# A fp32r decoder trunk on one core: 32 bytes more per buffer of the weights' parts and per block of the normed activations

## The chip, the core and the metric

The kernel runs on one core of one Trainium2 chip. The metric is the device time of one execution in microseconds. Before the change the median of three runs is 1750.88 us (1750.79 to 1751.33). One more execution was taken with the hardware profiler, and every row below is from it.

## The reference

Two identical layers (DEPTH = 2) on one sequence of 512 tokens, model width 1024, in float32:

```
for l in range(DEPTH):
    h = rms_norm(x, ln1[l])
    x = x + mixer_block(h, ...)      # one input projection, four token mixers, gated up-projections, w_out
    h = rms_norm(x, ln2[l])
    x = x + swiglu(h, w_ffn_in[l], w_ffn_out[l])
...
def swiglu(h, w_in, w_out):
    gate, up = jnp.split(h @ w_in, 2, axis=-1)
    return (jax.nn.silu(gate) * up) @ w_out
```

Nearly all arithmetic is in the products with weights: the input projection of 8,220 columns, the up-projections, `w_out`, and the feed-forward part with 2,816 hidden units.

## The kernel before

Activations lie transposed: 128 partitions hold 128 channels, and the 512 tokens run along the partition. A weight matrix is cut into blocks of 128 x 128, and eight blocks make a slab of 128 x 1024 float32, 4,096 bytes in each partition. SyncE's queue brings a slab into a tile `wr`. `convert` splits it into two parts: ScalarE copies it, rounded to fp32r, into `wh` (line 197), and VectorE subtracts, so that `wl` holds the rest (line 198). Activations are split in the same manner: `Norm` holds the normed activations as `xh` and `xl`, eight blocks of 512 columns each; other operands are split into tiles `t` (mixers) and `f` (feed-forward part).

Each product is three matmuls (`mm3`, all recorded under line 183): high by high, low activations by high weights, high activations by low weights. A matmul has a stationary operand, here nearly always a 128 x 128 weight block, and a moving operand, here the activations' columns. TensorE loads the stationary operand of the next matmul (a row of PEld) while the moving operand of the present one streams. For the token-major projections the roles are exchanged: blocks of `xh` and `xl` are stationary, and 256 or 284 columns of `wh` and `wl` move.

The order of the work is that of the program text with fillers pulled in between the mixers' steps, put in order once when the kernel is built. Slabs are split two ahead of their use (`AHEAD`). The first feed-forward product goes by Strassen's seven products on halves of 256 columns: the moving operands are halves of `xh` and `xl` and sums `t1`, `t2`, `t3` in tiles of their own. For three of the seven (p = 1, 2, 4) both weights' parts are in `wh` and `wl` (`wl` by an accumulating DMA from GpSimd's queue, lines 1263 and 1264). For the other four the low part is in a tile `l`.

Where a buffer lies follows from the pools, which are laid one behind the other in the order of the code, each buffer with its bytes per partition. Of the addresses, the remainder modulo 128 matters here; it is called the phase. Before the change every buffer that is named below has a length that is a multiple of 128 bytes, and so:

| buffers | role in TensorE | phase before | phase after |
|---|---|---|---|
| `wh`, three buffers | mostly stationary | 64, 64, 64 | 64, 96, 0 |
| `wl`, three buffers | mostly stationary | 64, 64, 64 | 32, 64, 96 |
| `xh`, `xl`, block k of eight | mostly moving | 64 for all k | 32k: 0, 32, 64, 96, 0, ... |
| `t`, `f`, `t1`, `t2`, `t3` | moving | 0 | 0 |
| `l` | stationary | 0 | 0 |
| `wr` | read by ScalarE, VectorE | 64 | 64 |

A block of 128 weight columns is 512 bytes, so all eight blocks of a slab have the slab's phase. Buffers rotate, so that `wl` lies 32 below its `wh` as long as both advance together.

Of the kernel before, what the change touches and what calls it, by code (L numbers as in the profile page):

```python
# [10 lines left out]
F32 = mybir.dt.float32  # L11
F32R = mybir.dt.float32r
# [6 lines left out]
P = 128  # L19
S = 512  # L20
D = 1024
KD = D // P
# [13 lines left out]
SLAB = 8  # L36
# [95 lines left out]
def trunk(ctx: ExitStack, tc: tile.TileContext, keys, qkeys, xin, pos, wst, wsq, par, ext, cst, out):  # L132
# [4 lines left out]
    wp = ctx.enter_context(tc.tile_pool(name="wp", bufs=3))  # L137
    bp = ctx.enter_context(tc.tile_pool(name="bp", bufs=1))
# [7 lines left out]
    def nm(s):  # L146
        uid[0] += 1
        return f"{s}{uid[0]}"

    pools = {}  # L150

    def phase(**bufs):
        st = ExitStack()
        for n, b in bufs.items():
            pools[n] = st.enter_context(tc.tile_pool(name=nm(n), bufs=b, reuse_waits="tile"))
        return st

    def mixers():
        return phase(gp=2, vp=2, bd=1, tp=33)
# [7 lines left out]
    def FT(shape, dtype=F32):  # L167
        return pools["fp"].tile(shape, dtype, tag="f", name=nm("f"))
# [27 lines left out]
    def split(src, hi, lo):  # L196
        A.copy(out=hi, in_=src)  # L197
        V.tensor_tensor(out=lo, in0=src, in1=hi.bitcast(F32), op=ALU.subtract)  # L198
        return hi, lo
# [38 lines left out]
    def halves(n):  # L238
        w = SLAB * P
        return [slice(0, w // 2), slice(w // 2, w)] if n < 2 else [slice(0, w)]  # L240

    def convert():
        n = len(ready)
        if n < SLABS:
            hi = wp.tile([P, SLAB * P], F32R, tag="wh", name=nm("wh"))
            lo = wp.tile([P, SLAB * P], F32R, tag="wl", name=nm("wl"))
            for h in halves(n):
                split(raw[n][:, h], hi[:, h], lo[:, h])
            ready.append((hi, lo))
            raw[n] = None  # L250

    def ahead(n):
        while len(ready) < min(SLABS, cap[0], n):
            if len(raw) == len(ready):
                load()
            convert()
# [105 lines left out]
    class Norm:  # L362
        def __init__(self, gain):
            self.gain = gain
            self.hi = bp.tile([P, KD, S], F32R, tag="xh", name=nm("xh"))
            self.lo = bp.tile([P, KD, S], F32R, tag="xl", name=nm("xl"))
            self.part = []

        def __getitem__(self, k):
# [51 lines left out]
    def layer(l, n1, scope):  # L421
# [770 lines left out]


        scope = phase(tq=1, ep=8, rp=5, lp=2, fp=9)

        last = l == DEPTH - 1
# [33 lines left out]
        def strassen(units):  # L1230
            n = len(units)
            st = [{} for _ in units]
# [8 lines left out]
            def load(u):  # L1241
                for q, (dk, dm) in (("11", (0, 0)), ("12", (HK, 0)), ("21", (0, 1)), ("22", (HK, 1))):
                    if q == "22":
                        t = wp.tile([P, SLAB * P], F32, tag="wr", name=nm("wr"), bufs=2)
                    else:
                        t = pools["rp"].tile([P, SLAB * P], F32, tag="rq", name=nm("rq"))
                    j = len(qkeys) // SLAB
                    for base in (0, FFN):
                        qkeys.extend([("w_ffn_in", l, k + dk, base + (units[u] + dm) * P) for k in range(HK)])
                    nc.sync.dma_start(out=t, in_=wsq[j])  # L1250
                    st[u][q] = t, j

            def sub(o, a, b, op=ALU.subtract):
                V.tensor_tensor(out=o, in0=a, in1=b, op=op)
                return o

            def LT():
                return pools["lp"].tile([P, SLAB * P], F32R, tag="l", name=nm("l"))

            def early(u, p):  # L1260
                t, j = st[u][OF[p]]
                lo = wp.tile([P, SLAB * P], F32R, tag="wl", name=nm("wl"))
                A.activation(out=lo, in_=t, func=AF.Copy, scale=-1.0)  # L1263
                G.dma_start(out=lo, in_=wsq[j], accum_op=ALU.add)  # L1264
                st[u]["lo", p] = lo

            def prep(u, p):
                s = st[u]
                hi = wp.tile([P, SLAB * P], F32R, tag="wh", name=nm("wh"))
                if p in LATE:  # L1270
                    A.copy(out=hi, in_=s[OF[p]][0])
                    s[p] = hi, s.pop(("lo", p))
                    return
                a11, a12, a21, a22 = (s[q][0] for q in ("11", "12", "21", "22"))
                if p == 6:
                    s1 = wp.tile([P, SLAB * P], F32, tag="wr", name=nm("wr"), bufs=2)
                    s["s1"] = sub(s1, a21, a22, ALU.add)
                    sub(a21, a11, a21)
                    sub(a11, s1, a11)
                    s[p] = split(a11, hi, LT())  # L1280
                    if u + 1 < len(units):
                        load(u + 1)
                    return
                if p == 3:
                    sub(a12, a12, a11)
                t = {5: s["s1"], 7: a21, 3: a12}[p]
                s[p] = split(t, hi, LT())
# [10 lines left out]
            def begin(i):  # L1298
                if i < 0:
                    load(0)  # L1300
                    upto("early", 2, early, lambda p: p in LATE)
                    return
                upto("prep", i + 3, prep, lambda p: True)
                upto("early", i + 6, early, lambda p: p in LATE)
# [80 lines left out]
        hi, lo = split(a, FT([P, 2, S], F32R), FT([P, 2, S], F32R))  # L1385
# [117 lines left out]
```

## Time and profile before

| | |
|---|---|
| median of three runs | 1750.88 us |
| the profiled execution, its own time | 1751.48 us |
| its span, first to last instruction | 1749.8 us |
| TensorE matmuls busy | 1736.9 us, 99% of the span |
| weight loads (PEld) busy | 1500.2 us, 86% |
| VectorE, ScalarE, GpSimd busy | 1215.5, 862.0, 225.9 us |

Matmuls are recorded with modelled ends: the recorded duration of one covers more than the time until the next starts, because they are pipelined. The time that a stream of matmuls costs is read from the starts: last start less first start, over the number of matmuls between them.

### The profile page before, as it was taken

What the parts mean: (1) busy time and instruction counts of PE and PEld (TensorE: products, weight loads), DVE (VectorE), ACT (ScalarE), POOL (GpSimd) and SP (SyncE); (2) the same over time, 40 slices, a digit from 0 to 9 for tenths busy, and PEclk for the clock granted to TensorE, in tenths of its full rate; (3) what the DMA queues carried; (4) which work ended last, traced back from release to release, by engine and by line L of the source; (5) the groups of instructions that cost most, each with busy time, mean ns of one, the idle gap of its engine ahead of it and who ended that gap; (6) DMA issues with size and microseconds to landing.
All of it is one profiled execution on the core that took longest, in us unless ns stands there. A gap on an engine that the chain in (4) does not pass through costs nothing.

```text
span 1749.8 us, 25123 instructions
## 1 busy us (share of the span) xinstructions
PE 1736.9 (99%) x10140; PEld 1500.2 (86%) x10140; DVE 1215.5 (69%) x1683; ACT 862.0 (49%) x1190; POOL 225.9 (13%) x227
## 2 busy tenths in 40 slices
PE   9999999999999999999999999999999999999998
PEld 7878888888888999898988788888888898999987
DVE  5868576777667666675777666767776685666666
ACT  5425533555347455463544254335544473645543
POOL 2032120022101000000010311201220010100000
PEclk9999999999999999999999999999999999999999
DMA  6322222222236566575333222322222365656652
GB/s 202 97 83 62 86 72 85 84 85 85 84 97 171 157 140 172 130 183 108 86 102 114 68 67 73 96 73 84 85 84 85 119 169 146 147 156 140 173 107 99
DMA packets 54693, 195.00 MB, mean 111 GB/s; under 512 B 6064, under 2 KB 6448, under 8 KB 54576
## 3 DMA queue, kind: packets, MB, share of 16 engines
q1 hardware_dynamic: 45072, 160.45, 29.0%
q0 software_dynamic: 8640, 31.46, 10.4%
q8 instruction: 79, 1.29, 0.3%
q10 hardware_dynamic: 864, 1.48, 0.2%
q14 instruction: 38, 0.31, 0.1%
HBM read 191.27 MB, written 2.10 MB: 111 GB/s over the span
## 4 chain that ended last, share of the span: by engine, by line
PE 96%; DVE 2%; DMA 1%; ACT 1%; issue 0%; ACTq 0%; DVEq 0%
PE mm L183 64%; PE mx L183 31%; DVE wl L198 1%; PE mx L1058 0%; DMA x<-in_x_dram 0%; DMA t<-in_ext_dram 0%; ACT wh L197 0%; DVE f L1399 0%; DVE x L1400 0%; PE mx L658 0%; DVE t L352 0%; ACT L216 0%; ACT g L221 0%; DVE t L1147 0%; PE mx L930 0%
## 5 line engine op out<-in xcount | busy, mean ns | idle before, releaser
L197 ACT CAST wh<-wr 128x1024 fp32r<-128x1024 f32 (+1 forms) x240 | 249.8, 1042 | 394.5 <-PE mm L183 247.7
L183 PE MATMUL mm<-xh,wh 128*128 128x512 f32 (+1 forms) x1184 | 431.4, 364 | 0.8 <-DVE t L1147 0.8
L183 PE MATMUL mm<-xh,wl 128*128 128x512 f32 (+1 forms) x1184 | 430.5, 364 | 0.0
L183 PE MATMUL mm<-xl,wh 128*128 128x512 f32 (+1 forms) x1184 | 429.8, 363 | 0.0
L198 DVE TENSOR_TENSOR wl<-wr,wh 128x1024 fp32r<-128x1024 f32 (+1 forms) x220 | 282.0, 1283 | 117.9 <-ACT wh L197 109.7
L183 PEld LDWEIGHTS mm<-xh,wh 128*128 128x128 f32 x1184 | 223.5, 189 | 36.3 <-DVE t L1147 1.7
L183 PEld LDWEIGHTS mm<-xh,wl 128*128 128x128 f32 x1184 | 223.7, 189 | 34.8 <-issue 1.5
L183 PEld LDWEIGHTS mm<-xl,wh 128*128 128x128 f32 x1184 | 223.6, 189 | 33.7 <-issue 1.1
L183 PE MATMUL mm<-t,wh 128*128 128x512 f32 x448 | 142.5, 397 | 0.0
L183 PE MATMUL mx<-xl,wh 128*128 128x256 f32 (+1 forms) x448 | 140.4, 313 | 0.0
L183 PE MATMUL mx<-xh,wh 128*128 128x256 f32 (+1 forms) x448 | 137.8, 314 | 2.3 <-ACT wh L197 2.3
L1264 POOL DMA_DIRECT2D wl<-in_wsq_dram x60 | 51.9, 864 | 542.1 <-ACT wl L1263 322.9
L183 PE MATMUL mx<-f,wh 128*128 128x512 f32 x352 | 110.2, 395 | 0.0
L183 PE MATMUL mm<-f,wh 128*128 128x512 f32 x352 | 108.3, 396 | 0.0
L183 PEld LDWEIGHTS mm<-t,wh 128*128 128x128 f32 x448 | 83.2, 188 | 19.1
L198 DVE TENSOR_TENSOR l<-rq,wh 128x1024 fp32r<-128x1024 f32 x60 | 73.2, 1220 | 34.6 <-ACT wh L197 19.1
L183 PEld LDWEIGHTS mx<-xh,wh 128*128 128x128 f32 x448 | 84.6, 189 | 8.9 <-ACT wh L197 3.5
L183 PE MATMUL mx<-xh,wl 128*128 128x256 f32 (+1 forms) x288 | 91.9, 330 | 0.0
L183 PEld LDWEIGHTS mx<-xl,wh 128*128 128x128 f32 x448 | 84.7, 189 | 5.3
L183 PE MATMUL mm<-t,wl 128*128 128x512 f32 x224 | 88.5, 395 | 0.0
L183 PEld LDWEIGHTS mm<-f,wh 128*128 128x128 f32 x352 | 65.7, 188 | 16.2 <-ACT wh L197 1.0
L183 PEld LDWEIGHTS mx<-f,wh 128*128 128x128 f32 x352 | 65.4, 188 | 15.5
(275 smaller groups left out, 3470.8 us busy)
## 6 DMA issues: line engine op xcount, KB each, us to landing
wr<-in_wst_dram SPq DMA_DIRECT2D x216, 512.0 KB, 3.5
rq<-in_wsq_dram SPq DMA_DIRECT2D x60, 512.0 KB, 4.6
wl<-in_wsq_dram POOLq DMA_DIRECT2D x60, 512.0 KB, 5.7
wr<-in_wsq_dram SPq DMA_DIRECT2D x20, 512.0 KB, 5.0
out_dram<-x SPq DMA_DIRECT2D x8, 256.0 KB, 2.0
x<-in_x_dram SPq DMA_DIRECT2D x3, 512.0 KB, 6.9
wr<-in_wst_dram SPq DMA_DIRECT2D x4, 256.0 KB, 5.4
x<-in_x_dram SPq DMA_DIRECT2D x2, 256.0 KB, 4.5
```

The costliest lines, as they stand in the source:

```text
L183: T.matmul(o, lhsT=l, rhs=r, start=start, stop=stop, skip_group_check=True)
L197: A.copy(out=hi, in_=src)
L198: V.tensor_tensor(out=lo, in0=src, in1=hi.bitcast(F32), op=ALU.subtract)
L1264: G.dma_start(out=lo, in_=wsq[j], accum_op=ALU.add)
```

## The change

Every buffer of `wh` and `wl` becomes 8 float32 (32 bytes) longer, and every block of `xh` and `xl` too; the additional elements are neither written nor read, since the slices `[:, :SLAB * P]` and `[:, :, :S]` cut them off. A tile of 64 bytes is laid in front of each phase's pools, which brings the buffers behind it back to the phase that they had. The built program has the same instructions on every engine, in the same order, with the same waits; only addresses differ.

```diff
+    def pad(pool, n):
+        pool.tile([P, n // 4], F32, tag=nm("pad"), name=nm("pad"))
+
...
     def phase(**bufs):
         st = ExitStack()
+        pad(st.enter_context(tc.tile_pool(name=nm("gap"), bufs=1)), 64)
...
     def convert():
...
-            hi = wp.tile([P, SLAB * P], F32R, tag="wh", name=nm("wh"))
-            lo = wp.tile([P, SLAB * P], F32R, tag="wl", name=nm("wl"))
+            hi = wp.tile([P, SLAB * P + 8], F32R, tag="wh", name=nm("wh"))[:, :SLAB * P]
+            lo = wp.tile([P, SLAB * P + 8], F32R, tag="wl", name=nm("wl"))[:, :SLAB * P]
...
     class Norm:
...
-            self.hi = bp.tile([P, KD, S], F32R, tag="xh", name=nm("xh"))
-            self.lo = bp.tile([P, KD, S], F32R, tag="xl", name=nm("xl"))
+            self.hi = bp.tile([P, KD, S + 8], F32R, tag="xh", name=nm("xh"))[:, :, :S]
+            self.lo = bp.tile([P, KD, S + 8], F32R, tag="xl", name=nm("xl"))[:, :, :S]
```

In the feed-forward part, `early` and `prep` take their `wl` and `wh` tiles with the same 8 more elements.

## Rows read from the trace of the kernel before

**Rows 1.** The page's busy times and the chain that ended last.

```profile
PE 1736.9 (99%) x10140; PEld 1500.2 (86%) x10140; DVE 1215.5 (69%) x1683; ACT 862.0 (49%) x1190; POOL 225.9 (13%) x227
...
PE 96%; DVE 2%; DMA 1%; ACT 1%; issue 0%; ACTq 0%; DVEq 0%
```

**Rows 2.** Span and granted TensorE clock.

```profile
core 0: 1749.8 us, clock 0.999
```

**Rows 3.** TensorE's groups by form: out<-moving,stationary xcount | busy, mean ns | idle before.

```profile
L183 PE MATMUL mm<-xh,wh 128*128 128x512 f32 x864 | 340.7, 394 | 0.8 <-DVE t L1147 0.8
...
L183 PE MATMUL mm<-t,wh 128*128 128x512 f32 x448 | 142.5, 397 | 0.0
...
L183 PE MATMUL mm<-f,wh 128*128 128x512 f32 x352 | 108.3, 396 | 0.0
...
L183 PE MATMUL mm<-xh,wh 128*128 128x256 f32 x320 | 90.6, 283 | 0.0
...
L183 PE MATMUL mx<-xh,wh 128*128 128x256 f32 x320 | 90.5, 283 | 0.0
...
L183 PE MATMUL mx<-xh,wh 128*128 128x512 f32 x128 | 47.3, 394 | 2.3 <-ACT wh L197 2.3
...
L183 PE MATMUL mx<-xh,l 128*128 128x256 f32 x160 | 44.5, 278 | 0.0
...
L183 PE MATMUL mm<-t2h,wh 128*128 128x256 f32 x160 | 44.5, 283 | 0.0
...
L183 PE MATMUL mx<-t,wh 128*128 128x512 f32 x128 | 40.5, 394 | 0.0
L183 PE MATMUL mm<-wl,xh 128*128 128x256 f32 x128 | 36.6, 286 | 0.0
```

**Rows 4.** Line 183, 530 to 545 us: xcount: duration ns min/median/max, first to last start.

```profile
L183 PE MATMUL mx<-xh,wh x23: 388/390/395, 529.8 to 544.8; 128*128 128x512 f32 x23
L183 PE MATMUL mx<-xl,wh x23: 389/389/397, 530.0 to 545.0; 128*128 128x512 f32 x23
L183 PE MATMUL mx<-xh,wl x22: 389/390/390, 530.2 to 544.5; 128*128 128x512 f32 x22
```

**Rows 5.** Line 183, 508 to 528 us, moving operand `t`.

```profile
L183 PE MATMUL mm<-t,wh x59: 393/394/395, 507.6 to 527.9; 128*128 128x512 f32 x59
L183 PE MATMUL mm<-t,wl x29: 394/394/395, 507.8 to 527.4; 128*128 128x512 f32 x29
```

**Rows 6.** Line 183, 855 to 876 us, moving operand `f`.

```profile
L183 PE MATMUL mx<-f,wh x31: 394/394/396, 854.8 to 869.5; 128*128 128x512 f32 x31
```

**Rows 7.** TensorE's timeline, 569.4 to 577 us, matmuls of 256 columns: start, duration.

```profile
569.50 0.28 PE L183 MATMUL mx<-xh,l 128*128 128x256 f32 x1
...
570.56 0.28 PE L183 MATMUL mx<-xh,l 128*128 128x256 f32 x1
...
570.91 0.28 PE L183 MATMUL mm<-xh,wl 128*128 128x256 f32 x1
...
572.35 0.28 PE L183 MATMUL mm<-xh,wl 128*128 128x256 f32 x1
...
575.89 0.28 PE L183 MATMUL mm<-t2h,l 128*128 128x256 f32 x1
...
576.95 0.28 PE L183 MATMUL mm<-t2h,l 128*128 128x256 f32 x1
```

**Rows 8.** Line 183, 65.5 to 77.9 us: weights move, 284 columns.

```profile
L183 PE MATMUL mx<-wh,xh x32: 290/294/302, 65.5 to 77.7; 128*128 128x284 f32 x32
L183 PE MATMUL mx<-wl,xh x32: 290/294/298, 65.6 to 77.8; 128*128 128x284 f32 x32
L183 PE MATMUL mx<-wh,xl x31: 292/293/298, 65.7 to 77.5; 128*128 128x284 f32 x31
```

**Rows 9.** TensorE's timeline, 950 to 953 us: a stream of `x` after other work.

```profile
950.78 0.39 PE L183 MATMUL mm<-xl,wh 128*128 128x512 f32 x1
...
952.16 0.39 PE L183 MATMUL mm<-xl,wh 128*128 128x512 f32 x1
```

More of the change, by code (lines that the diff above doesn't have):

```diff
@@ L1261, in early @@
                 t, j = st[u][OF[p]]
-                lo = wp.tile([P, SLAB * P], F32R, tag="wl", name=nm("wl"))
+                lo = wp.tile([P, SLAB * P + 8], F32R, tag="wl", name=nm("wl"))[:, :SLAB * P]
                 A.activation(out=lo, in_=t, func=AF.Copy, scale=-1.0)
@@ L1268, in prep @@
                 s = st[u]
-                hi = wp.tile([P, SLAB * P], F32R, tag="wh", name=nm("wh"))
+                hi = wp.tile([P, SLAB * P + 8], F32R, tag="wh", name=nm("wh"))[:, :SLAB * P]
                 if p in LATE:
```

## The prediction

> **What bounds the kernel now.** I read the page's busy times and its chain first, then the granted clock, then the groups of TensorE by form, and last single stretches of TensorE's line by their starts. [...] No other engine and no transfer has more than 2% of the chain. So only one thing can move the time: how far apart the matmuls start. What the change does to the buffers' addresses cannot lengthen anything else visibly: VectorE, ScalarE and GpSimd are idle for 31%, 51% and 87% of the span [rows 1] and split slabs two ahead of their use, and that lead covers a copy or a subtraction that became some per cent slower through its new address. If the cover were gone, one more tenth on the splits would cost TensorE waits, but nothing in the change takes it away: instructions, order and waits are the same.
>
> **What the spacing depends on now.** [...]
>
> - Moving `x`, stationary `w`, 512 columns [rows 4]: 68 matmuls, first start 529.8, last 545.0, so 15.2 us over 67 intervals: 226.9 ns.
> - Moving `t`, stationary `w`, 512 columns [rows 5]: 88 matmuls, 507.6 to 527.9, 20.3 us over 87: 233.3 ns. Moving `f` has the same recorded duration as `t`, 394 ns against 389 to 390 for `x` [rows 4 to 6], so I take 233.3 for it too.
> - 256 columns, moving `x`, both weights' parts in `wh` and `wl` [rows 7]: from 570.91 to 572.35 twelve intervals, 120.0 ns.
> - 256 columns, moving `x`, low part in `l`: from 569.50 to 570.56 nine intervals, 117.8 ns. Moving `t2`, low part in `l`: from 575.89 to 576.95 nine intervals, 117.8 ns [rows 7].
> - 284 columns, weights move, `x` stationary [rows 8]: 95 matmuls, 65.5 to 77.8, 94 intervals: 130.9 ns.
>
> Same engine, same clock, same form, same lines of code; what differs between the first two is which buffers are read. By the table of phases, call "relation" the stationary operand's phase less the moving one's, modulo 128, while the next weights load under the running stream. It is 0 in the first stream, 64 in the second, 0 in the third, and a mix of 0 and 64 in the fourth pair. In the fifth the moving columns start 1,136 bytes further for each of three row blocks, so the relation goes through 0, 16 and 32. [...]
>
> [...]
>
> **The change part by part.** The 32 bytes themselves cost nothing: no element more is moved, written or read, and the tile of 64 bytes is never touched. What the change does is to spread the relations. How many matmuls that concerns is in the groups [rows 3]:
>
> - 512 columns, moving `x`: 864 on `mm` and 128 on `mx`, each three times (high by high, low by high, high by low): 2976. Relation now 0. After: block k of `x` lies at 32k, so whatever the slab's phase, the eight blocks go twice through 0, 32, 64, 96.
> - 512 columns, moving `t` or `f`: 448 + 128 for `t` by `wh` and half as many by `wl` makes 864; `f` by `wh` is 352 on `mm`, as many on `mx`, half as many by `wl`: 1056. Together 1920. Relation now 64. After: 64, 96, 0 with `wh`, 32, 64, 96 with `wl`: 64 for a third.
> - 256 columns with relation 0 throughout: 320 three times on `mm`, on `mx` 320 high blocks less the 160 that go with `l`, three times: 1440; the token-major ones, 128 three times: 384. Together 1824. After: a mix.
> - 256 columns that have a mix already: `x` with `l`, 160 three times, and `t1` to `t3`, 160 nine times: 1920. After: another mix.
>
> Prices per matmul. Relations 0 and 64 stand in the rows: 226.9 and 233.3. [...] For 96 there is no row. Above, it is bounded by 233.3, the dearest settled one. [...]
>
> The sum:
>
> - `x`, 512: mean of 226.9, 226.9, 233.3, 226.9 is 228.5, so 1.6 ns more on 2976: +4.8 us.
> - `t` and `f`: one third at 233.3, two thirds at 226.9 makes 229.0, so 4.3 ns less on 1920: -8.2 us.
> - 256 columns, relation 0 until now: they become a mix, 120.0 to 117.8, 2.2 ns on 1824: -4.0 us.
> - 256 columns, mixed already: 0; bounds plus and minus 2.2 ns on 1920, 4.2 us either way. Between them nothing speaks for a side.
>
> Together -7.4 us. The profiled execution took 1751.5 us (span 1749.8 and 1.7 around it), which is 0.6 over the median; 1751.5 less 7.4 is 1744.1, and by the median 1743.5. The likeliest case reaches from -12 (the mixed 256-column ones gain their 4.2 us too) to -3 us (96 costs 230: then `x` is at 229.3, +7.1 us, `t` and `f` at 230, -6.3 us, together -3.2): 1739 to 1748.
>
> **The rivals.**
>
> *The spread is dearer than the settled state (slower).* Place: the 2976 matmuls with moving `x`. Such a stream after other work [rows 9]: six intervals, 950.78 to 952.16, are 230.0 ns each, with all relations 0 as in [rows 4]. So 226.9 is a state that the engine settles into when every matmul repeats the same phases. After the change the relation moves by 32 with every block k, that is after three matmuls, and by 32 between high and low part. If it never settles, `x` costs 230.0 or more: +3.1 on 2976 is +9.2 us; `t` and `f`, unsettled too, gain perhaps a ns, -2 us; the 256-column ones stay: +7.2 us, 1758. It decides once `x` passes 231 ns while `t`, `f` and the 256-column streams gain as in my sum (12.2 us over 2976 is 4.1 ns), or 227.6 ns if these gain only 2 us. For it: the unsettled intervals. Against: the mixed 256-column streams, which repeat a pattern of three and are not dearer.
>
> [...]
>
> *The change does nothing.* The 6.4 ns then come from something else that distinguishes `t` and `f` from `x`, such as the distance of the buffers, not their phase. 1750.9. For it: only two phases occur in the big streams, always with the same kinds of tiles.
>
> **How the numbers follow.** Chances: the forecast 0.37, much faster 0.16, nothing 0.18, slower 0.29. A measurement of this kernel can tell about 0.2%, 3.5 us, from no change. Most of the forecast's case lies beyond that, 0.33, and 0.04 within; so faster 0.49, same 0.22, slower 0.29. The range runs from 1722, a little under the much faster case, to 1761, where `x` unsettled costs 231 and nothing is gained elsewhere.
>
> **What would show each step right or wrong.** [...] Recorded durations should move alike, 389 and 394 towards each other. If TensorE's share of the chain falls, or waits on `wh` and `wl` grow, the change did something to the other engines that I priced at nothing. I am wrong above all if relation 96 is not like 32, or if settling matters more than the relation.

## The result and the profile after

The changed kernel takes 1758.3 us (median of five runs, 1758.16 to 1759.01) against 1750.93 before: ratio 1.0043, 95% interval 1.0029 to 1.0056. It is slower by 7.4 us; forecast was 7.4 us faster. The first rival had said 1758.

The page's busy times, the chain's shares by engine, and the groups of the two splits (line | busy, mean ns | idle before), then the same two groups in the kernel before:

```profile
PE 1745.5 (99%) x10140; PEld 1501.4 (85%) x10140; DVE 1215.3 (69%) x1683; ACT 861.9 (49%) x1190; POOL 225.9 (13%) x227
...
PE 96%; DVE 2%; DMA 1%; ACT 1%; issue 0%; SPq 0%; DVEq 0%; ACTq 0%
...
L201 ACT CAST wh<-wr 128x1024 fp32r<-128x1024 f32 (+1 forms) x240 | 249.5, 1041 | 402.0 <-PE mm L187 246.9
...
L202 DVE TENSOR_TENSOR wl<-wr,wh 128x1024 fp32r<-128x1024 f32 (+1 forms) x220 | 281.8, 1282 | 122.4 <-ACT wh L201 114.8
```

```profile
L197 ACT CAST wh<-wr 128x1024 fp32r<-128x1024 f32 (+1 forms) x240 | 249.8, 1042 | 394.5 <-PE mm L183 247.7
...
L198 DVE TENSOR_TENSOR wl<-wr,wh 128x1024 fp32r<-128x1024 f32 (+1 forms) x220 | 282.0, 1283 | 117.9 <-ACT wh L197 109.7
```

The span is 1757.3 us where [rows 1, 2] belong to 1749.8. VectorE's and ScalarE's busy times are the same within 0.2 us, the chain's share of TensorE is the same, the clock is again 0.999: only TensorE's own time has grown. Line 183 is now line 187. Two streams, read as [rows 4] and [rows 5] were (xcount: duration min/median/max, first to last start):

```profile
L187 PE MATMUL mx<-xl,wh x21: 390/394/402, 535.7 to 549.6; 128*128 128x512 f32 x21
L187 PE MATMUL mx<-xh,wl x21: 389/394/398, 535.9 to 549.9; 128*128 128x512 f32 x21
L187 PE MATMUL mx<-xh,wh x20: 389/397/400, 536.1 to 549.4; 128*128 128x512 f32 x20
...
L187 PE MATMUL mm<-t,wh x39: 391/394/399, 512.7 to 525.9; 128*128 128x512 f32 x39
L187 PE MATMUL mm<-t,wl x19: 392/394/398, 512.9 to 525.5; 128*128 128x512 f32 x19
```

Moving `x`: 62 matmuls over 14.2 us, 61 intervals of 232.8 ns (226.9 before). Moving `t`: 58 over 13.2 us, 231.6 (233.3 before). Note the spread too: 389 to 402 within a stream, where [rows 4] have 388 to 397 and medians of 389 to 390. And 256 columns with both weights' parts in `wh` and `wl`, in TensorE's timeline:

```profile
575.66 0.28 PE L187 MATMUL mm<-xh,wl 128*128 128x256 f32 x1
...
577.07 0.28 PE L187 MATMUL mm<-xh,wl 128*128 128x256 f32 x1
```

Twelve intervals in 1.41 us: 117.5 ns against 120.0 in [rows 7].

Over all matmuls of a class the account closes. For this and the table below I took, in each trace, the time from each start to the next, grouped by moving operand and columns. Summed over the 2976 with moving `x` at 512 columns it went from 689.6 to 701.1 us (+11.5), for `t` and `f` from 453.2 to 451.1 (-2.1), for `x` by `wh` or `wl` at 256 from 210.7 to 208.3 (-2.4), token-major from 46.7 to 45.9 (-0.8), the 256-column classes with a mix before +1.6. That is +7.8; the span grew by 7.5.

### The profile page after: what moved, and what is told of

Its sections match the earlier page's. It is cut to its first block, busy times and chain, and to the rows that moved or that the text cites. A ratio compares the mean times of both kernels' runs of the same rounds, so it can differ in the third digit from the quotient of the medians.

```text
span 1757.3 us, 25123 instructions
## 1 busy us (share of the span) xinstructions
PE 1745.5 (99%) x10140; PEld 1501.4 (85%) x10140; DVE 1215.3 (69%) x1683; ACT 861.9 (49%) x1190; POOL 225.9 (13%) x227
## 4 chain that ended last, share of the span: by engine, by line
PE 96%; DVE 2%; DMA 1%; ACT 1%; issue 0%; SPq 0%; DVEq 0%; ACTq 0%
PE mm L187 64%; PE mx L187 31%; DVE wl L202 1%; DMA wr<-in_wst_dram 1%; PE mx L1062 0%; DMA x<-in_x_dram 0%; ACT wh L201 0%; DVE f L1403 0%; DVE x L1404 0%; PE mx L662 0%; DVE t L356 0%; ACT L220 0%; ACT g L225 0%; DVE t L1151 0%; PE mx L934 0%
## 5 line engine op out<-in xcount | busy, mean ns | idle before, releaser
L201 ACT CAST wh<-wr 128x1024 fp32r<-128x1024 f32 (+1 forms) x240 | 249.5, 1041 | 402.0 <-PE mm L187 246.9
L202 DVE TENSOR_TENSOR wl<-wr,wh 128x1024 fp32r<-128x1024 f32 (+1 forms) x220 | 281.8, 1282 | 122.4 <-ACT wh L201 114.8
```

## The experiments

A stream settles when the spacing of its matmuls no longer changes, or changes in a pattern that repeats. Theory "settling", from the first rival: a stream has a cheap state only while each matmul repeats the phases of the one before it, and what it costs then depends on the relation. Rival "prices by relation", that of the prediction: each matmul has the price of its own relation, whatever its neighbours are. Second rival, "distance": the 6.4 ns between `x` and `t` come from the kind or place of the buffers. All kernels below are edits of the kernel before, not of the changed one, and differ from it in addresses alone. Mean interval in ns from start to start in each class (512 columns without intervals over 260 ns, 256 without those over 160, which I take for waits), and the times:

| kernel | x, 512 | t, 512 | f, 512 | x by wh/wl, 256 | median us | ratio to before, 95% interval |
|---|---|---|---|---|---|---|
| before | 228.0 | 233.3 | 233.4 | 119.7 | 1750.9 | |
| the change | 232.0 | 231.9 | 232.1 | 118.4 | 1758.3 | 1.0043 (1.0029 to 1.0056) |
| x_only | 232.5 | 233.0 | 233.3 | 118.3 | 1760.8 | 1.0054 (1.0037 to 1.007) |
| w_only | 232.1 | 232.0 | 232.2 | 118.2 | 1757.7 | 1.0037 (1.0025 to 1.005) |
| tf64 | 227.7 | 227.3 | 227.3 | 119.7 | 1739.1 | 0.9931 (0.9916 to 0.9946) |
| x_rel32 | 233.4 | 229.7 | 229.2 | 119.6 | 1759.4 | 1.0046 (1.0031 to 1.0061) |
| tf128 | 228.4 | 230.1 | 232.9 | 119.8 | 1749.4 | 0.9991 (0.9981 to 1.0) |
| tf192 | 228.1 | 232.6 | 232.5 | 119.7 | 1749.8 | 0.9994 (0.9984 to 1.0003) |
| x_r96_tf_r32 | 233.9 | 233.3 | 233.2 | 117.7 | 1764.8 | 1.008 (1.0065 to 1.0095) |
| w_128 | 232.0 | 231.9 | 232.0 | 119.1 | 1758.7 | 1.0044 (1.0028 to 1.0061) |
| w_256 | 228.0 | 233.3 | 233.4 | 119.7 | 1751.1 | 1.0 (0.9991 to 1.0009) |
| tf320 | 227.7 | 227.3 | 227.3 | 119.8 | 1739.3 | 0.9932 (0.9916 to 0.9949) |
| lo32 | 232.5 | 231.5 | 231.7 | 118.6 | 1757.6 | 1.0037 (1.0024 to 1.005) |
| r224 | 233.2 | 233.2 | 233.3 | 117.2 | 1761.8 | 1.006 (1.004 to 1.0081) |

### Each half of the change alone

x_only:

```diff
-            self.hi = bp.tile([P, KD, S], F32R, tag="xh", name=nm("xh"))
+            self.hi = bp.tile([P, KD, S + 8], F32R, tag="xh", name=nm("xh"))[:, :, :S]
```

and the same for `xl`. 

> Only the blocks of the normed activations are 32 bytes longer (phases 64, 96, 0, 32, ...); the weights' parts stay at 64. Settling (a stream is cheap only while each matmul repeats the phases of the one before): moving x at 512 columns leaves 227 ns for 231 to 232, +9 to +12 us, its 256-column streams fall from 120 to 118.5, -2.5 us, moving t and f stay at 233.3 ns; 1757 to 1760 us. Prices by relation, as in the prediction (0 and 32 and 96 at 226.9, 64 at 233.3): x at 228.5, +4.8 us, 256 columns -4 us; 1751 to 1752 us.

w_only, with a tile of 64 bytes ahead of `xh`, so that `x` keeps its phase:

```diff
-            hi = wp.tile([P, SLAB * P], F32R, tag="wh", name=nm("wh"))
+            hi = wp.tile([P, SLAB * P + 8], F32R, tag="wh", name=nm("wh"))[:, :SLAB * P]
```

and the same for `wl` and for both tiles of the feed-forward part. 

> Only the weights' parts are 32 bytes longer (64, 96, 0 and 32, 64, 96); x stays at 64 and t, f at 0. Within a slab the phases now repeat in a pattern of three matmuls. Settling, if it needs the very same phase in every matmul: x at 512 columns 231 to 232 ns, +9 to +12 us, t and f 232, -2 us, 256 columns -3 us; 1755 to 1758 us. Settling, if a repeated pattern of three is enough: x stays near 227 in most slabs; 1745 to 1750 us. Prices by relation: x 228.5, t and f 229.0, as predicted; 1743 to 1745 us.

Moving `x` in x_only, then in w_only:

```profile
L183 PE MATMUL mx<-xh,wh x21: 388/396/402, 535.8 to 549.8; 128*128 128x512 f32 x21
L183 PE MATMUL mx<-xl,wh x21: 387/394/399, 536.1 to 550.0; 128*128 128x512 f32 x21
L183 PE MATMUL mx<-xh,wl x20: 388/394/398, 536.3 to 549.5; 128*128 128x512 f32 x20
```

```profile
L185 PE MATMUL mx<-xl,wh x21: 390/393/399, 535.6 to 549.5; 128*128 128x512 f32 x21
L185 PE MATMUL mx<-xh,wl x21: 392/392/397, 535.8 to 549.8; 128*128 128x512 f32 x21
L185 PE MATMUL mx<-xh,wh x20: 389/397/398, 536.1 to 549.3; 128*128 128x512 f32 x20
```

Both have 61 intervals over 14.2 us, 232.8 ns. Either half takes the cheap state from `x`, and both together cost no more than one: 1757.7 and 1760.8 against 1758.3. x_only is the dearer by 3.1 us: its `t` and `f` keep 233 ns, which is 1.7 us of it, and its `x` takes 232.5 instead of 232.1, which is 1.2; w_only has the whole of the change's loss. Prices by relation (1751 to 1752, 1743 to 1745) is refuted in both.

### Equal phases for t and f

tf64; `phase()` lays a gap ahead of the two pools alone:

```diff
     pools = {}
+    GAP = {'tp': 64, 'fp': 64}
...
         for n, b in bufs.items():
+            if n in GAP:
+                st.enter_context(tc.tile_pool(name=nm("gap"), bufs=1)).tile([P, GAP[n] // 4], F32, tag=nm("pad"), name=nm("pad"))
```

> Nothing is spread; the pools of t and f alone are laid 64 bytes later, so that t and f have phase 64 like the weights' parts, relation 0. If the relation of settled streams sets their spacing: moving t and f fall from 233.3 to 227 to 228 ns, 1920 matmuls, -10 to -12 us; 1739 to 1741 us. If the distance or the kind of buffer makes the 233.3: no change, 1751 us.

```profile
L186 PE MATMUL mm<-t,wh x39: 389/389/390, 512.9 to 525.9; 128*128 128x512 f32 x39
L186 PE MATMUL mm<-t,wl x20: 389/389/390, 512.7 to 525.6; 128*128 128x512 f32 x20
```

59 matmuls, 58 intervals over 13.2 us: 227.6 ns, and all durations 389 to 390, as in [rows 4] and unlike the 394 of [rows 5]. 64 bytes of address turn 233.3 into 227.3 on 1920 matmuls: 6.0 ns, 11.5 us, and the time falls by 12 us. "Distance" is refuted, and this version, which spreads nothing and makes everything alike, beats both kernels.

### Other relations, and the modulus

x_rel32 lays 96 bytes ahead of `xh` and 32 behind `xl`:

```diff
+    gb = ctx.enter_context(tc.tile_pool(name="gb", bufs=1))
+    gb.tile([P, 24], F32, tag="gb", name="gb")
     bp = ctx.enter_context(tc.tile_pool(name="bp", bufs=1))
+    ga = ctx.enter_context(tc.tile_pool(name="ga", bufs=1))
+    ga.tile([P, 8], F32, tag="ga", name="ga")
```

> Nothing is spread; x is laid 32 bytes lower modulo 128 (phase 32), so that its relation is 32 in all streams with the weights' parts. Prices by relation as predicted: 226.9 ns as at relation 0, 1751 us. Settling with a level of its own for each relation: some step between 220 and 233 ns, the same for all of the stream; at 220 -20 us (1731), at 233.3 +16 us (1767).

Moving `x`, then moving `t`:

```profile
L187 PE MATMUL mx<-xh,wh x21: 392/394/395, 535.6 to 549.6; 128*128 128x512 f32 x21
L187 PE MATMUL mx<-xl,wh x21: 399/399/400, 535.8 to 549.8; 128*128 128x512 f32 x21
L187 PE MATMUL mx<-xh,wl x20: 392/392/392, 536.1 to 549.4; 128*128 128x512 f32 x20
...
L187 PE MATMUL mm<-t,wh x37: 392/392/395, 513.6 to 526.0; 128*128 128x512 f32 x37
L187 PE MATMUL mm<-t,wl x18: 388/388/389, 514.1 to 525.8; 128*128 128x512 f32 x18
```

Relation 32 was the one that I had priced at 226.9: it is 233.4, +8.1 us in the end. The stream does repeat, in threes: the place in the group of three decides the duration (394, 399, 392). And `t` went to 229.7 without having moved modulo 128. All that lies behind `x` had moved by 128 bytes, so 128 is not the modulus. Five kernels on that:

tf128, tf192 and tf320 are tf64 with another gap:

```diff
-    GAP = {'tp': 64, 'fp': 64}
+    GAP = {'tp': 128, 'fp': 128}
```

> Nothing is spread; t and f are laid 128 bytes later, so modulo 128 nothing changes (relation to the weights 64), modulo 256 their relation goes from 64 to 192. If the phase counts modulo 128, as the change has it: t and f stay at 233.3 ns, 1751 us. If it counts modulo 256 or more: they go to the 229.4 ns that they had, without being touched, in the run with x at phase 32, where all that lies behind x had moved by 128 bytes; 1920 matmuls, -7.5 us, 1743 to 1744 us.

> Nothing is spread; t and f are laid 192 bytes later: relation 0 modulo 128, as in the run with 64 bytes, but 128 modulo 256. Modulo 128: 227.3 ns again, 1739 us. Modulo 256: a level of its own, between 220 (1725 us) and 233.4 ns (1751 us).

> Nothing is spread; t and f are laid 320 bytes later, relation 0 modulo 256 and 256 modulo 512. Phase modulo 256: 227.3 ns as with 64 bytes, 1739 us. Phase modulo 512: another level, between 229 and 233.4 ns, 1743 to 1751 us.

w_128 and w_256 are w_only with 32 and 64 more elements instead of 8 (128 and 256 bytes):

```diff
-            hi = wp.tile([P, SLAB * P], F32R, tag="wh", name=nm("wh"))
+            hi = wp.tile([P, SLAB * P + 32], F32R, tag="wh", name=nm("wh"))[:, :SLAB * P]
```

> The weights' buffers are spread as in the run with the weights alone, but by 128 bytes instead of 32, so that modulo 128 all stay at 64. If the phase counts modulo 128: all streams settle as before, 1751 us. If it counts modulo 256: high and low part and successive slabs differ by 128, the streams do not settle or settle on another level, x at 512 columns 229 to 232 ns; 1750 to 1758 us.

> The weights' buffers are spread by 256 bytes instead of 32 or 128; modulo 256 all stay as before, modulo 512 they alternate. If the phase counts modulo 256: every stream settles as before, x at 512 columns 228.0 ns, 1751 us; that also would show that longer and spread buffers cost nothing by themselves. If it counts modulo 512 or more: 231 to 232 ns and 1757 to 1759 us, as with 32 and 128.

Moving `x` in w_128, in w_256; moving `t` in tf192, in tf320:

```profile
L183 PE MATMUL mx<-xl,wh x21: 395/396/397, 535.7 to 549.6; 128*128 128x512 f32 x21
L183 PE MATMUL mx<-xh,wl x21: 393/397/398, 536.0 to 549.9; 128*128 128x512 f32 x21
L183 PE MATMUL mx<-xh,wh x20: 389/389/394, 536.2 to 549.4; 128*128 128x512 f32 x20
```

```profile
L183 PE MATMUL mx<-xh,wh x23: 388/389/395, 529.8 to 544.8; 128*128 128x512 f32 x23
L183 PE MATMUL mx<-xl,wh x22: 389/389/398, 530.1 to 544.4; 128*128 128x512 f32 x22
L183 PE MATMUL mx<-xh,wl x22: 389/389/390, 530.3 to 544.6; 128*128 128x512 f32 x22
```

```profile
L186 PE MATMUL mm<-t,wh x38: 392/395/398, 513.0 to 525.8; 128*128 128x512 f32 x38
L186 PE MATMUL mm<-t,wl x19: 392/392/398, 512.8 to 525.4; 128*128 128x512 f32 x19
```

```profile
L186 PE MATMUL mm<-t,wh x40: 389/389/389, 512.8 to 525.9; 128*128 128x512 f32 x40
L186 PE MATMUL mm<-t,wl x19: 389/389/389, 513.2 to 525.5; 128*128 128x512 f32 x19
```

Spreading the weights by 128 bytes costs as much as by 32 (232.0 ns); spreading them by 256 costs nothing (228.0, ratio 1.0). A shift of `t` and `f` by 192 bytes, equal phases modulo 128, does not find the cheap state (232.5); 64 and 320, equal modulo 256, do (227.3). So in these runs the phase counts modulo 256, and longer, scattered buffers cost nothing as long as it stays (w_256, 1751.1 us against 1750.9). tf128 was a miss in part: `t` 230.1, `f` 232.9 where 229.4 was expected, and 1749.4 us, which cannot be told from no change. In x_rel32 `f` has the same phases as here and 229.2, so the relation alone does not fix the spacing here.

x_r96_tf_r32 and r224 lay gaps ahead of `xh`, behind `xl` and ahead of the pools of `t` and `f` as above (160, 96 and 32 bytes; 32, 224 and 96 bytes), so that the remaining multiples of 32 modulo 256 are measured. 

> Nothing is spread; x lies at relation 96 and t, f at relation 32 to the weights, both modulo 256. Prices by relation modulo 128 as in the prediction: 226.9 ns for both, t and f -12 us, 1739 us. Settling with a level for each relation: two levels of their own, of which no row tells; at relation 160 (which is 32 modulo 128) x had 233.4 ns, and if t, f have that here and x 229, 1753 us.

> Nothing is spread; x, t and f all lie at relation 224 modulo 256 to the weights, the one multiple of 32 that no other run has. If relation 0 is the one cheap relation: 512 columns settle or not at 229 to 234 ns for all of them, x +1 to +6 ns on 2976, t and f 0 to -4 ns on 1920; 1750 to 1768 us. If there is a second cheap one here: 227 ns or less for all, 1739 us or less.

Moving `x` in the one, in the other:

```profile
L190 PE MATMUL mx<-xh,wh x18: 392/398/400, 537.4 to 549.4; 128*128 128x512 f32 x18
L190 PE MATMUL mx<-xl,wh x18: 392/394/400, 537.7 to 549.6; 128*128 128x512 f32 x18
L190 PE MATMUL mx<-xh,wl x18: 391/397/400, 537.9 to 549.8; 128*128 128x512 f32 x18
```

```profile
L190 PE MATMUL mx<-xh,wh x20: 393/395/397, 536.3 to 549.6; 128*128 128x512 f32 x20
L190 PE MATMUL mx<-xl,wh x20: 393/395/397, 536.5 to 549.8; 128*128 128x512 f32 x20
L190 PE MATMUL mx<-xh,wl x19: 393/396/397, 536.8 to 549.4; 128*128 128x512 f32 x19
```

53 intervals over 12.4 us are 234.0 ns, 58 over 13.5 are 232.8. With these two every relation modulo 256 in steps of 32 has been seen at 512 columns: 0 has 227 to 228 ns, 192 has 229 to 233, all others 232 to 234. Prices by relation had put x_r96_tf_r32 at 1739; it took 1764.8.

### One phase, or a pattern of three

lo32 lays 32 bytes between the high and the low weights' buffers once and 480 bytes ahead of `xh`, so that nothing else moves modulo 512:

```diff
             hi = wp.tile([P, SLAB * P], F32R, tag="wh", name=nm("wh"))
+            if n == 0:
+                wp.tile([P, 8], F32, tag="wg", name=nm("wg"), bufs=1)
             lo = wp.tile([P, SLAB * P], F32R, tag="wl", name=nm("wl"))
```

> All weights' high parts stay where they are, all low parts are laid 32 bytes later, and nothing else moves modulo 512: each group of three matmuls now has two phases, the same in every group and slab. If settling needs one phase throughout: x at 512 columns 231 to 232 ns, +10 to +12 us, t and f about 232, -2 us, 256 columns -2 us; 1757 to 1759 us. If it needs only that groups of three repeat: a settled pattern of three, its mean anywhere between 226.7 and 233.4 ns but the spacings repeat every third matmul; 1745 to 1765 us.

TensorE's timeline in a stream of moving `x`:

```profile
542.02 0.40 PE L185 MATMUL mx<-xh,wh 128*128 128x512 f32 x1
542.25 0.40 PE L185 MATMUL mx<-xl,wh 128*128 128x512 f32 x1
542.49 0.39 PE L185 MATMUL mx<-xh,wl 128*128 128x512 f32 x1
542.72 0.40 PE L185 MATMUL mx<-xh,wh 128*128 128x512 f32 x1
...
543.42 0.40 PE L185 MATMUL mx<-xh,wh 128*128 128x512 f32 x1
```

Here it settles: every group of three takes 0.70 us, 542.02 to 542.72 to 543.42. But it settles at 233.3 ns, 6.4 above the state with one phase. So repetition by itself is not what makes a stream cheap, and "settling" in my first wording falls as well. The three matmuls do not share the loss alike. Over the whole kernel high by high takes 232.0 ns on the mean, low by high 236.2 and high by low 229.4, where before the three took 228.0, 228.1 and 227.8. The dearest is the one under which the shifted low part is loaded (in the kernel before, low by high and the load of the next `wl` both start at 542.27 us), and high by high is dearer although it and the one after it touch only buffers at equal phases.

## Why the prediction was wrong

**What bounds the kernel, and what the 32 bytes cost.** Right. TensorE's spacing is the only thing that moved; ScalarE's and VectorE's splits are as long as before (1041 and 1282 ns against 1042 and 1283), and w_256 shows buffers longer by 256 bytes at a ratio of 1.0.

**Phases, not distance.** Right, and shown by tf64 and tf320. An edit of addresses alone moved 1920 matmuls by 6.0 ns each, from 233.3 to 227.3.

**The prices.** The step that failed: 226.9 for relations 32 and 96 in the sum, and the mean over four relations that was built on it. That 226.9 was an estimate of mine, and no run shows it: the lowest mean at 512 columns at any relation other than 0 was 229.2 (`f` in x_rel32). Three things were wrong in the step. First, the prices: the relations that stood for 32 and 96 settle at 233 to 234 ns (x_rel32, x_r96_tf_r32, r224). The nearest row, the 284-column stream at relations 0, 16 and 32 [rows 8], is another form, and it did not move at all: its sum was 25.2 us before and after. Second, the modulus: it is 256, not the 128 by which the table of phases counts, so what I called four relations were eight, of which one is cheap at 512 columns. Third, the mean itself: in the changed kernel a matmul with moving `x` whose own relation is 0 modulo 128 takes 231.5 ns on the mean of 702 intervals, one with relation 64 takes 232.4 on 724, where the prediction had 226.9 and 233.3. In lo32 the high by high matmuls keep relation 0, for their own weights and for the next ones, and still go from 228.0 to 232.0. So a matmul has no price by its own relation here; the stream around it sets the price too.

**The terms.** The measured ones are the sums of the account above. `x` at 512: forecast +4.8 us, measured +11.5. `t` and `f`: forecast -8.2, measured -2.1. The 256-column ones with relation 0: forecast -4.0, measured -3.2, of which about -2.7 falls to the 1824 that the forecast counted (the class in the account takes in 320 more, `x` by `wh` in streams with `l`); about two thirds of that term came. Mixed already: forecast 0, measured +1.6 in the other 1600, within the 4.2 given. The upper end of the range, 1761, does not follow from its own premise: 231 ns for `x` is 4.1 ns on 2976, 12.2 us, and that makes 1763; nothing else hangs on it. The lower end, 1722, and the chance of much faster rest on 220 ns for relations 32 and 96, an estimate of mine too (226.9 less the 6.4 between `x` and `t`, rounded); no run shows it, and at these relations `x`, `t` and `f` took 233.2 to 233.9.

**The rival that came true.** It named the place (moving `x`), the price (230 or more, measured 232.0) and the time (1758). That the time agrees so well is partly luck: `x` cost 11.5 us where it said 9.2, and the 256-column streams, which it left as they were, gave back 1.6. Its reason holds in this form: what the spread destroys is the state that `x` and the weights had by lying at equal phases. That a stream is cheap because it repeats does not hold (lo32).

**What stays open.** Why 256 bytes, and what in the chip has that period: the runs show when it costs, not what does. Why relation 192 gave 229 and 230 ns in three classes and 233 in a fourth. Whether equality is all that a cheap stream needs: in every kernel with one the weights kept the remainder modulo 256 that they had before, and no run laid weights and moving operand together at another. And whether the 256-column streams, which are cheapest at other relations (117.2 in r224 against 119.7), could be given one of their own; it was not tried.

## What to carry to other kernels

Where TensorE is the bound and its operands are float32 columns, measure the time from start to start of each stream, and compare it between streams of one form: a difference of 2.6% (233.3 against 227.3 ns) came from addresses alone here. In this kernel the only cheap streams of 512 columns were those with the moving operand and the weights at the same remainder modulo 256 in every matmul; a gap of 64 bytes ahead of two pools gave 0.7%, and spreading the remainders took 0.4%. A mean of prices was a poor forecast here, where neighbours decide a price (228.5 against 232.0 ns for `x`): undo the change for one operand first.

## What the runs showed of the hardware that was not expected

- The spacing of a stream of 512 columns depended here on the addresses of the weights and of the moving operand, and came back after 256 bytes in a partition: with the weights' buffers spread by 32 or 128 bytes moving `x` takes 232.1 and 232.0 ns (w_only, w_128), by 256 bytes 228.0 (w_256), as before; with `t` and `f` laid 64 or 320 bytes later these take 227.3 (tf64, tf320), 192 bytes later 232.5 (tf192).
- At 512 columns equal phases are the best case: 227.3 to 228.4 ns, against 229 to 234 for the seven other relations. At 256 columns they are not the best: moving `x` by `wh` or `wl` takes 119.7 ns at equal phases, and 117.2 (r224), 117.7 (x_r96_tf_r32) and 119.6 (x_rel32) at the three other relations that were held throughout.
- A stream can settle on a pattern of three (lo32, x_rel32) at a mean of 233 ns, which is no less than what `x` takes in the changed kernel, where the relations change from block to block (232.0).
